# Two fixed PSUM tiles for the divided projections, and the recurrence's key columns scaled on VectorE

## The chip, the cores and the metric

The kernel runs on one core of one Trainium2 chip. The core has five engines that run their own instruction streams and meet at semaphores: TensorE (PE in the profile; its weight loads are listed apart as PEld), VectorE (DVE), ScalarE (ACT), GpSimd (POOL) and SyncE (SP), which here issues transfers. The metric is the device time of one execution in microseconds (us), lower is better; the figure compared is the median of several runs.

## The reference

One inference step of a one-layer streaming encoder for 512 prompt frames and 32 frames of a running stream, all in fp32. What matters here is the HGRN2 half of the mixer:

```
proj = x @ w_in                                  # hq, hf, hi, hg: 8 heads of 128 columns each
f = lb + (1 - lb) * sigmoid(hf);  k = 1 - f      # forget gate and key
S_t = diag(f_t) S_{t-1} + k_t outer v_t          # v = hi
o_t = S_t^T q_t                                  # q = hq
o = rms_norm(o) * silu(hg)
...                                              # latent attention, w_out, ConvFFN with w_up, w_gate, w_down
```

## The kernel before, in words

All activations stand with features on the 128 partitions and the T = 544 frames along the free dimension. An fp32 product is made from three reduced-precision passes: a weight is split into a high part `wh` (ACT copy) and a low part `wl` (DVE subtraction), an activation into `aH` and `aL`, and `wh*aH`, `wh*aL`, `wl*aH` are added up in PSUM.

The projections of heads 2 to 7 are **divided**: the two column groups of a call (query and forget gate, or value and gate, 128 columns each), the two halves of the 2048 input features and the two halves of the frames (NI = 272) make a 2x2x2 block product, done with seven products instead of eight. A call of `divided` (L749) runs the products in the order `ORDER` = 11, s1, s2, s4, s3, 12, 22. Each is 8 k-tiles x 3 passes = 24 matmuls of 272 columns, about 3 us of PE. There are 12 calls, c = 4 to 15 (an even c is a head's query and forget gate, the next odd c its value and gate). Products 11, s2, s3, 22 accumulate into `x`, products s1, s4, 12 into `y`, so consecutive products always alternate between the two. Each accumulator's running value is **taken** (`take`, L755) after each product: for 11, s1, s2 and 22 by an ACT copy (L758), for s4, s3 and 12 by a DVE addition (L761). `x` and `y` are the two halves, each in a 2 KB PSUM bank of its own, of one tile [128, 1024] that `main_tile()` gives anew in each call; there are two such buffers, so calls alternate between them.

The order of work on PE, DVE and ACT is written out by hand in this stage (`tc.manual_schedule`, L948); GpSimd's and SyncE's is not. Per product, in program order: ACT makes `wh` of the product after next (`begin`, L716), PE runs k = 0 to 3, then `settle()` issues the take of the *previous* product, then DVE makes `wl` of the product after next (L721) and often a difference of two weight blocks for the one after that (L711), then a **slot** opens for side work, PE runs k = 4 to 7, and a second slot opens. So a call has 14 slots, a head 28.

The side work is the recurrence of the head before. `levels(h)` (nine steps, about every 1.75 slots) does a doubling scan with block widths m = 1, 2, ..., 64: at each level PE multiplies the scaled keys `Kp` with the scaled queries `Qp` into a PSUM tile `s` (L836 to L841), then the upper half blocks of `Qp` are multiplied by the block totals on DVE (L842), the lower half blocks of `Kp` on GpSimd (L844), the totals are multiplied pairwise on DVE (L850), and the masked scores are copied on DVE (L854) or ACT (L852). The next level's matmuls need the new `Qp` and `Kp`. `finish(h)` (11 steps, one per slot) transposes keys and values (L870), builds the states (L880 to L894), multiplies (L902, L904), squares on ACT (L907), sums on DVE (L911, L912), takes a power on GpSimd (L913), scales on DVE (L916), transposes back (L921) and gates (L923, L925). For heads 0 and 1 the projections are ordinary GEMMs and the same `levels` is woven into them (L939, L940), there outside the hand-written order.

Of the kernel before, what the change touches and what calls it, by code (L numbers as in the profile page):

```python
# [15 lines left out]
P = 128  # L16
# [26 lines left out]
NI = T // 2  # L43
# [16 lines left out]
def tile_encoder_step(ctx, tc, xp, xs, w_in, w_in4, w_kr, w_q_b, w_kv_b, w_out, w_up, w_gate, w_down, w_down2,  # L60
# [3 lines left out]
    V, A, G, PE = nc.vector, nc.scalar, nc.gpsimd, nc.tensor  # L64
# [27 lines left out]
    def main_tile():  # L92
        return psm.tile([P, 1024], F32, name="main", tag="main")
# [54 lines left out]
    def pair_half(ps, j):  # L148
        n = H_[j].stop - H_[j].start
        return [ps[:, 512 * t:512 * t + n] for t in range(2)]  # L150
# [213 lines left out]
    with tc.tile_pool(name="mp", bufs=1) as mp, tc.tile_pool(name="psa", bufs=4, space=PSUM) as psa:  # L364
# [67 lines left out]
        c = {}  # L432
# [207 lines left out]
    with tc.tile_pool(name="gp", bufs=1) as gp, tc.tile_pool(name="psg", bufs=1, space=PSUM) as psg:  # L640
# [83 lines left out]
        def operand(name, k):  # L724
            if name in sums:
                return part(name, k, 0), part(name, k, 1)
            kg, j = {"11": (k, 0), "s3": (k, 1), "12": (HK + k, 0), "22": (HK + k, 1)}[name]
            return aH[kg][:, H_[j]], aL[kg][:, H_[j]]
# [4 lines left out]
        def begin(n):  # L733
            if n < len(products):
                ws_of[n] = products[n][0].high(products[n][1])

        def complete(n):

            if n < len(products):
                ws_of[n] = products[n][0].low(ws_of[n])  # L740
                if n + 1 < len(products):
                    products[n + 1][0].form(products[n + 1][1])

        def settle():
            now, later[:] = later[:], []
            for f in now:
                f()

        def divided(c, a, b, after):  # L749

            ps = main_tile()
            x, y = ps[:, :NI], ps[:, 512:512 + NI]
            t0, t1 = H_

            def take(name, out):  # L755
                kept = {"11": a[:, t0], "s1": b[:, t1], "s2": b[:, t0], "22": a[:, t1]}.get(name)
                if kept is not None:
                    A.activation(kept, out, AF.Copy)  # L758
                else:
                    z = {"s4": b[:, t0], "s3": b[:, t1], "12": a[:, t0]}[name]  # L760
                    V.tensor_tensor(out=z, in0=z, in1=out, op=ALU.add)  # L761
                    if name != "12":
                        after(z)

            for i, name in enumerate(ORDER):
                n = 7 * (c - N_PLAIN) + i
                begin(n + 2)
                wh, wl = ws_of.pop(n)
                out = x if name in ("11", "s2", "s3", "22") else y
                for k in range(HK):  # L770
                    oh, ol = operand(name, k)
                    for q, (ww, aa) in enumerate(((wh, oh), (wh, ol), (wl, oh))):
                        PE.matmul(out, ww[:, k * P:(k + 1) * P], aa, start=name in ("11", "s1", "12") and k == 0 and q == 0,  # L773
                                  stop=k == HK - 1 and q == 2, skip_group_check=True)
                    if k == 3:
                        settle()
                        complete(n + 2)
                        yield
                later.append(lambda name=name, out=out: take(name, out))
                yield  # L780
# [4 lines left out]
        def divided_qf(h):  # L785
            q, f = hq[h], hf[h] = proj_tile(), proj_tile()

            def forget(z):
                A.activation(z, z, AF.Sigmoid)
                A.activation(z, z, AF.Identity, bias=lb[:, h:h + 1], scale=oml[:, h:h + 1])  # L790
            yield from divided(2 * h, q, f, forget)

        def divided_ig(h):
            i, g = hi[h], hgate[h] = proj_tile(), proj_tile()

            def gate(z):
                e = gp.tile([P, 2, NI], F32, name="sg", tag="sg")[:, 0]
                A.activation(e, z, AF.Sigmoid)
                later.append(lambda: V.tensor_tensor(out=z, in0=z, in1=e, op=ALU.mult))
            yield from divided(2 * h + 1, i, g, gate)  # L800

        def sw_tile():
            return psg.tile([P, 1024], F32, name="sw", tag="sw")

        def s1_tile():
            return psg.tile([P, 512], F32, name="s1", tag="s1", bufs=2)

        def levels(h):
            q, f = hq[h], hf[h]
            at = attnT[h % 2]  # L810
            s0 = gp.tile([P, P], F32, name="s0", tag="s0", bufs=2)
            dma(s0, st_d[h])
            Kp = gp.tile([P, T], F32, name="Kp", tag="Kp", bufs=2)
            Qp = gp.tile([P, T], F32, name="Qp", tag="Qp", bufs=2)
            V.tensor_scalar(out=Kp, in0=f, scalar1=-1.0, scalar2=1.0, op0=ALU.mult, op1=ALU.add)
            V.tensor_tensor(out=Qp, in0=q, in1=f, op=ALU.mult)
            yield
            dps = sw_tile()
            for j, (a, b) in enumerate(TOK):
                t0 = a if j < 4 else TP  # L820
                PE.matmul(dps[:, t0:b], Kp[:, a:b], q[:, t0:b], start=True, stop=True)
            V.copy_predicated(out=at, mask=hm[:, :T], data=dps[:, :T])
            tot = f
            tots = None
            for li, m in enumerate(LEVELS):
                n = T if m <= 16 else TP
                nb = n // (2 * m)
                Qv = Qp[:, :n].rearrange("p (b w m) -> p b w m", w=2, m=m)
                Kv = Kp[:, :n].rearrange("p (b w m) -> p b w m", w=2, m=m)
                Av = at[:, :n].rearrange("p (b w m) -> p b w m", w=2, m=m)  # L830
                Tv = tot[:, :n // m].rearrange("p (b w) -> p b w", w=2)
                ps = s1_tile()
                bt = 64 // m
                for j, (a, b) in enumerate(TOK[:5 if m <= 16 else 4]):
                    if m == 64:
                        PE.matmul(ps[:64, j * 64:(j + 1) * 64], Kp[:, a:a + 64], Qp[:, a + 64:b], start=True, stop=True)  # L836
                    elif j < 4:
                        PE.matmul(ps[:, j * 64:(j + 1) * 64], Kp[:, a:b], Qv[:, j * bt:(j + 1) * bt, 1, :],  # L838
                                  start=True, stop=True)
                    else:  # L840
                        PE.matmul(ps[:, 256:272], Kp[:, a:b], Qv[:, 4 * bt:nb, 1, :], start=True, stop=True)  # L841
                V.tensor_tensor(out=Qv[:, :, 1, :], in0=Qv[:, :, 1, :], in1=Tv[:, :, 0:1].to_broadcast([P, nb, m]),  # L842
                                op=ALU.mult)
                G.tensor_tensor(out=Kv[:, :, 0, :], in0=Kv[:, :, 0, :], in1=Tv[:, :, 1:2].to_broadcast([P, nb, m]),  # L844
                                op=ALU.mult)
                if m == 16 or m == 64:
                    nt = gp.tile([P, 32], F32, name="totk", tag=f"tot{m}", bufs=2)
                else:
                    nt = gp.tile([P, 272], F32, name="tot", tag="tot", bufs=2)
                V.tensor_tensor(out=nt[:, :nb], in0=Tv[:, :, 0], in1=Tv[:, :, 1], op=ALU.mult)  # L850
                if m == 64:
                    A.activation(Av[:64, :, 1, :], ps[:64, :256].rearrange("p (b m) -> p b m", m=m), AF.Copy)  # L852
                else:
                    V.copy_predicated(out=Av[:, :, 1, :],  # L854
                                      mask=hm[:, T + 272 * li:T + 272 * li + n // 2].rearrange("p (b m) -> p b m", m=m),
                                      data=ps[:, :n // 2].rearrange("p (b m) -> p b m", m=m))
                if m == 16:
                    tots = nt
                tot = nt
                yield  # L860
            rec[h] = Kp, Qp, tot, tots, at, s0
# [82 lines left out]
        for n in range(2):  # L944
            begin(n)
            complete(n)
        last_finish = finish(HEADS - 1)
        with tc.manual_schedule(engines=MANUAL):  # L948

# [50 lines left out]
    def acc_tile():  # L1000
        seq[0] += 1
        if seq[0] % 2:
            return main_tile()
        return psA.tile([P, 1024], F32, name="acc", tag="acc")
# [349 lines left out]
    for g in (5, 6, 7):  # L1354
# [3 lines left out]
        if g < 7:  # L1358
            ps = pair_half(acc_tile(), 0)
# [218 lines left out]
    with tc.manual_schedule():  # L1578
# [26 lines left out]
        ps = pair_half(acc_tile(), 0)  # L1605
# [81 lines left out]
        for p in range(2, BP):  # L1687
            x = Pair(p)
# [553 lines left out]
```

## Time and profile before

| | |
|---|---|
| median of 3 runs | 2451.21 us (2450.78 to 2453.78) |
| profiled execution, its own time | 2452.24 us |
| its span, first to last instruction | 2450.5 us |
| PE busy | 2354.3 us (96% of the span) |
| DVE busy | 1812.1 us (74%) |
| ACT busy | 1045.2 us (43%) |
| POOL busy | 191.5 us (8%) |
| mean granted TensorE clock | 0.991 |

The own time has 1.7 us that lie outside the span; the profiled execution is 1.0 us above the median. Busy time is the union of an engine's instruction rows; PE rows overlap, because matmuls are pipelined. The divided stage, which the change is about, lies between 380.7 and 775.7 us of the span.

### The profile page before, as it was taken

The numbers are of one execution on the slowest core, as the hardware profiler recorded it, in microseconds if no ns is written. First come the engines' busy times: TensorE is split into PE (matmuls) and PEld (weight loads), VectorE is DVE, ScalarE is ACT, GpSimd is POOL, SyncE is SP. The second block draws the span as 40 slices with busy tenths as digits, with TensorE's granted clock in tenths as the row PEclk, the third lists the DMA queues.
The fourth block names the chain that finished last, engine by engine and source line by source line (L and its number), as shares of the span: only waits on it lengthen the run. The fifth ranks groups of instructions, "written<-read, shape, count | busy, mean of one in ns | idle before, by whom it ended". The sixth has DMA issues, their size and how long they took to land.

```text
span 2450.5 us, 44455 instructions
## 1 busy us (share of the span) xinstructions
PE 2354.3 (96%) x18462; PEld 2317.5 (95%) x18462; DVE 1812.1 (74%) x2447; ACT 1045.2 (43%) x1615; POOL 191.5 (8%) x219
## 2 busy tenths in 40 slices
PE   6999999888899999989999999999999999999997
PEld 6999999888888999989999999999999999999996
DVE  7445577666667546799888888888777888888566
ACT  4244433333334224656555555555444433333234
POOL 4010020111111020000000000000000100000023
PEclk9999999999999999999999999999999999999998
DMA  7232163222224433644535253534333874633322
GB/s 231 91 97 65 62 200 95 70 77 69 73 76 145 170 101 124 204 135 161 174 119 184 102 191 112 177 127 164 117 117 118 313 300 170 224 133 94 115 70 74
DMA packets 131914, 333.21 MB, mean 136 GB/s; under 512 B 11904, under 2 KB 64896, under 8 KB 127104
## 3 DMA queue, kind: packets, MB, share of 16 engines
q1 hardware_dynamic: 122448, 286.91, 35.6%
q0 software_dynamic: 5040, 39.00, 4.0%
q10 hardware_dynamic: 4224, 4.46, 0.5%
q8 instruction: 145, 2.38, 0.4%
q14 instruction: 57, 0.47, 0.1%
HBM read 272.78 MB, written 56.15 MB: 134 GB/s over the span
## 4 chain that ended last, share of the span: by engine, by line
PE 75%; DVE 6%; ACT 2%; issue 2%; POOL 0%; DMA 0%; ACTq 0%; SPq 0%; DVEq 0%
PE main L1217 20%; PE acc L1217 16%; PE main L773 9%; PE main L1245 8%; PE main L118 7%; PE acc L1245 6%; PE acc L118 5%; PE s L838 1%; DVE wl L1169 1%; ACT hproj L758 1%; ACT wh L716 0%; DVE wl L721 0%; DVE hproj L761 0%; ACT zb L1337 0%; PE sw L902 0%
## 5 line engine op out<-in xcount | busy, mean ns | idle before, releaser
L1168 ACT ACTIVATE wh<-raw 128x1024 fp32r<-128x1024 f32 x340 | 359.9, 1059 | 415.0 <-DVE raw L1161 134.4
L1169 DVE TENSOR_TENSOR wl<-raw,wh 128x1024 fp32r<-128x1024 f32 x340 | 415.8, 1223 | 133.9 <-ACT wh L1168 133.0
L1217 PE MATMUL main<-op,wh 128*128 128x272 f32 x1408 | 265.7, 288 | 0.0
L1217 PE MATMUL acc<-ops,wh 128*128 128x272 f32 x1344 | 255.7, 289 | 4.3 <-DVE ops L1298 4.3
L1217 PE MATMUL main<-ops,wh 128*128 128x272 f32 x1344 | 254.2, 287 | 0.0
L1217 PEld LDWEIGHTS main<-op,wh 128*128 128x128 f32 x1408 | 221.0, 188 | 0.0
L1217 PEld LDWEIGHTS acc<-ops,wh 128*128 128x128 f32 x1344 | 212.1, 189 | 4.6 <-DVE ops L1298 4.6
L1217 PEld LDWEIGHTS main<-ops,wh 128*128 128x128 f32 x1344 | 211.0, 188 | 0.0
L1217 PE MATMUL main<-op,wl 128*128 128x272 f32 x704 | 203.1, 288 | 0.9 <-DVE wl L1169 0.9
L1217 PE MATMUL acc<-ops,wl 128*128 128x272 f32 x672 | 194.3, 289 | 0.0
L1217 PE MATMUL main<-ops,wl 128*128 128x272 f32 x672 | 193.8, 288 | 0.2 <-DVE wl L1169 0.2
L118 PE MATMUL main<-aL,wh 128*128 128x272 f32 (+2 forms) x768 | 180.1, 292 | 4.6 <-POOL aL L269 4.6
L118 PE MATMUL main<-aH,wh 128*128 128x272 f32 (+2 forms) x768 | 183.4, 296 | 1.1 <-ACT x L267 0.7
L118 PE MATMUL main<-aH,wl 128*128 128x272 f32 (+2 forms) x768 | 178.9, 291 | 0.0
L107 DVE TENSOR_TENSOR wl<-raw,wh 128x1024 fp32r<-128x1024 f32 (+2 forms) x80 | 89.9, 1127 | 102.9 <-ACT wh L106 97.9
L1217 PE MATMUL acc<-op,wh 128*128 128x272 f32 x832 | 159.8, 290 | 1.6 <-DVE eg L1441 1.6
L1168 ACT ACTIVATE wh<-rawl 128x1024 fp32r<-128x1024 f32 x93 | 98.5, 1060 | 105.8 <-DVE rawl L1161 42.1
L1161 DVE TENSOR_TENSOR raw<-raw,raw 128x1024 f32<-128x1024 f32 x114 | 139.2, 1221 | 1.8 <-DMA raw<-in_w_up 0.2
L773 PE MATMUL main<-aH,wh 128*128 128x272 f32 x384 | 118.2, 308 | 22.6 <-DVE hproj L761 22.6
L1169 DVE TENSOR_TENSOR wl<-rawl,wh 128x1024 fp32r<-128x1024 f32 x93 | 113.8, 1223 | 32.7 <-ACT wh L1168 32.4
L106 ACT ACTIVATE wh<-raw 128x1024 fp32r<-128x1024 f32 (+2 forms) x80 | 75.5, 949 | 140.2 <-PE acc L118 65.6
L118 PEld LDWEIGHTS main<-aL,wh 128*128 128x128 f32 x768 | 129.6, 191 | 5.8 <-POOL aL L269 5.7
(421 smaller groups left out, 6162.0 us busy)
## 6 DMA issues: line engine op xcount, KB each, us to landing
raw<-in_w_in SPq DMA_DIRECT2D x76, 512.0 KB, 3.6
raw<-in_w_up SPq DMA_DIRECT2D x72, 512.0 KB, 4.6
raw<-in_w_gate SPq DMA_DIRECT2D x72, 512.0 KB, 4.0
raw<-in_w_down SPq DMA_DIRECT2D x71, 512.0 KB, 4.1
raw<-in_w_out SPq DMA_DIRECT2D x40, 512.0 KB, 3.5
opd<-ohl SPq DMA_DIRECT2D x16, 1088.0 KB, 5.5
ops<-opd POOLq DMA_DIRECT2D x16, 1088.0 KB, 9.7
opd<-ohl SPq DMA_DIRECT2D x16, 816.0 KB, 6.4
```

The lines of the kernel that those rows point to most:

```text
L106: A.activation(dst(hv), src(rv), AF.Copy)
L107: V.tensor_tensor(out=dst(lv), in0=src(rv), in1=dst(hv).bitcast(F32), op=ALU.subtract)
L118: PE.matmul(ps, ww[:, wcols[0]:wcols[1]], aa[:, hs[j]], start=first and i == 0, stop=last and i == 2, skip_group_check=True)
L758: A.activation(kept, out, AF.Copy)
L773: PE.matmul(out, ww[:, k * P:(k + 1) * P], aa, start=name in ("11", "s1", "12") and k == 0 and q == 0, stop=k == HK - 1 and q == 2, skip_g ...
L838: PE.matmul(ps[:, j * 64:(j + 1) * 64], Kp[:, a:b], Qv[:, j * bt:(j + 1) * bt, 1, :], start=True, stop=True)
L1161: V.tensor_tensor(out=out, in0=a, in1=b, op=ALU.subtract)
L1168: A.activation(wh, src, AF.Copy)
L1169: V.tensor_tensor(out=wl, in0=src, in1=wh.bitcast(F32), op=ALU.subtract)
L1217: PE.matmul(ps, ww[:, k * P:(k + 1) * P], aa, start=self.first and k == 0 and i == 0, stop=k == n - 1 and i == 2, skip_group_check=True)
L1245: PE.matmul(banks[:, 512 * u:512 * u + NI], ww[:, (u * n + k) * P:(u * n + k + 1) * P], aa, start=self.first and k == 0 and i == 0, stop=k ...
```

## The change

```diff
         def divided(c, a, b, after):
-            ps = main_tile()
-            x, y = ps[:, :NI], ps[:, 512:512 + NI]
+            x, y = (banks[(c + i) % 2][:, :NI] for i in range(2))
             t0, t1 = H_
...
                 V.tensor_tensor(out=Qv[:, :, 1, :], in0=Qv[:, :, 1, :], in1=Tv[:, :, 0:1].to_broadcast([P, nb, m]),
                                 op=ALU.mult)
-                G.tensor_tensor(out=Kv[:, :, 0, :], in0=Kv[:, :, 0, :], in1=Tv[:, :, 1:2].to_broadcast([P, nb, m]),
+                V.tensor_tensor(out=Kv[:, :, 0, :], in0=Kv[:, :, 0, :], in1=Tv[:, :, 1:2].to_broadcast([P, nb, m]),
                                 op=ALU.mult)
...
         for n in range(2):
             begin(n)
             complete(n)
+        banks = [main_tile() for i in range(2)]
         last_finish = finish(HEADS - 1)
```

Two things change. First, the accumulators of all 12 calls are the first halves of two tiles that are allocated once, ahead of the stage. `x` of call c is in tile c mod 2 and `y` in the other, so `x` and `y` of one call stand in different tiles, and the bank that holds `y` in one call holds `x` in the next; products alternate between the two banks across the calls too. Second, the multiplication of `Kp` at each level (L844) is a DVE instruction, between the multiplication of `Qp` (L842) and that of the totals (L850); `Kv[:, :, 0, :]` are the lower half blocks of `Kp`. Nothing else moves: the number of matmuls, the transfers and the order of the other instructions in the hand-written stage stay.

## Prediction

> **What bounds the kernel now.** First the page, for the bounding engine, then the stage of the change by windows, then its waits, last single rows in order of time.
>
> ```profile
> PE 2354.3 (96%) x18462; PEld 2317.5 (95%) x18462; DVE 1812.1 (74%) x2447; ACT 1045.2 (43%) x1615; POOL 191.5 (8%) x219
> 380.70:775.70 395.00, 353.03 (x2748) 338.55 (x2746) 271.60 (x388) 143.14 (x214) 53.10 (x49) 0.99 0.27 84
> PE main L773 <- DVE hproj L761: 22.6, 23, 2.5
> PE main L773 <- ACT hproj L758: 17.9, 31, 1.0
> ```
>
> PE is busy 96% of the span, so time comes only from PE's idle stretches or from a shorter stream. In the divided stage (second line: length, then PE, PEld, DVE, ACT, POOL busy, clock) PE idles 42.0 of 395 us, and the two waits, in microseconds, count and longest, make 40.5 of that: 54 times PE's next product matmul waits for a take. Which take, the rows tell:
>
> ```profile
> 480.54 0.41 PE L773 MATMUL main<-s,wh 128*128 128x272 f32 x2
> 480.79 0.29 PE L773 MATMUL main<-s,wl 128*128 128x272 f32 x1
> 481.11 0.40 ACT L758 ACTIVATE hproj<-main 128x272 f32<-128x272 f32 x1 [2.15 <-PE main L773]
> 481.56 0.52 PE L773 MATMUL main<-s,wh 128*128 128x272 f32 x2 [0.49 <-ACT hproj L758]
> 481.92 0.29 PE L773 MATMUL main<-s,wl 128*128 128x272 f32 x1
> 477.52 0.29 PE L773 MATMUL main<-aH,wh 128*128 128x272 f32 x1
> 477.64 0.37 ACT L758 ACTIVATE hproj<-main 128x272 f32<-128x272 f32 x1
> 477.65 0.29 PE L773 MATMUL main<-aL,wh 128*128 128x272 f32 x1
> ```
>
> The first five rows are the middle of product s1: PE has run k = 0 to 3 into `y`, ACT takes product 11 out of `x`. Two banks, no shared data, yet ACT starts only when PE's last matmul into `y` ends, having idled 2.15 us while 11 lay ready, and PE goes on only when ACT is done. The last three rows are the natural experiment: the take of 22 falls into the next call, whose 11 goes to the *other tile*, and PE does not pause. So the waits hang on the tile, not on the bank or the value.
>
> **The change part by part.** *Two tiles.* Neighbouring products then always stand in different tiles, as 22 and the next 11 do now, so the mid-product stop has nothing left to wait for. What one costs: 480.79 to 481.92 is 1.13 us for three matmuls that take 0.375 undisturbed (480.54 to 480.79 is two in 0.25, so 0.125 each). That is 0.755, 0.27 more than the 0.49 listed as idle, as the pipeline drains and refills. For 54 stops: 40.5 + 54 x 0.27 = 55.1 us.
>
> What is late next is the DVE chain that made the longest stops; they come once per head, five times:
>
> ```profile
> 474.24 0.40 PE L773 MATMUL main<-aH,wh 128*128 128x272 f32 x1 [2.50 <-DVE hproj L761]
> ...
> 740.44 0.40 PE L773 MATMUL main<-aH,wh 128*128 128x272 f32 x1 [2.51 <-DVE hproj L761]
> 466.45 0.71 ACT L907 ACTIVATE sqg<-sw 128x640 f32<-128x640 f32 x1 [2.76 <-PE sw L904]
> 467.06 1.05 ACT L716 ACTIVATE wh<-raw 128x1024 fp32r<-128x1024 f32 x1
> 468.32 1.22 DVE L721 TENSOR_TENSOR wl<-raw,wh 128x1024 fp32r<-128x1024 f32 x1
> 473.01 0.82 DVE L916 TENSOR_TENSOR sqg<-sw,r 128x640 f32<-128x640 f32 x1 [1.28 <-POOL r L913]
> 475.35 1.23 DVE L711 TENSOR_TENSOR raw<-raw 128x1024 f32<-128x1024 f32 x1
> 475.85 0.71 PE L921 MATMUL sw<-ident,sqg 128*128 128x128 f32 x5
> 476.31 0.37 PE L773 MATMUL main<-aH,wh 128*128 128x272 f32 x1
> 476.67 1.06 ACT L716 ACTIVATE wh<-raw 128x1024 fp32r<-128x1024 f32 x1 [4.78 <-DVE raw L711]
> 477.76 2.45 DVE L721 TENSOR_TENSOR wl<-raw,wh 128x1024 fp32r<-128x1024 f32 x2 [0.26 <-ACT wh L716]
> 481.27 0.43 DVE L815 TENSOR_SCALAR Kp<-hproj 128x544 f32<-128x544 f32 x1
> ```
>
> I set both chains at 466.2, where PE begins product 12, and run them on without the stops. DVE's weight subtraction cannot start before the ACT copy ends at 468.1, so the chain to L916 moves only 0.2 earlier and ends near 473.6. PE needs four half products of 12 x 0.125 = 1.5 us and is through 22 at 472.3; its transposes L921 read what L916 writes: a stop of 1.35. They take about 0.46 (475.85 to 476.31), so 11 runs from 474.1 to 477.15. Now s1 wants the bank that 22 filled, a wait the old alternation of tiles did not have. The take of 22 stands on ACT behind L716, which waits for L711: all 0.2 earlier than now, so done at 477.85, a stop of about 0.75. Product s1 ends at 480.9; the recurrence's first matmuls need `Kp` from L815, now at 481.1 to 481.5: 0.6 more. Put back: 2.7 per head, 13.5 for five.
>
> *`Kp` on DVE.* Rows of the divided stage, by shape (busy, mean ns of one, idle before):
>
> ```profile
> L844 POOL TENSOR_TENSOR Kp<-Kp,tot 128x272 f32<-128x272 f32 (+1 forms) x30 | 31.8, 1060 | 90.0 <-PE s L841 75.9 <-PE s L836 14.1
> L842 DVE TENSOR_TENSOR Qp<-Qp,hproj 128x272 f32<-128x272 f32 x6 | 2.7, 443 | 2.0 <-PE s L841 2.0
> L850 DVE TENSOR_TENSOR tot<-hproj 128x272 f32<-128x272 f32 x6 | 6.8, 1132 | 0.0
> L850 DVE TENSOR_TENSOR tot<-tot 128x136 f32<-128x136 f32 x6 | 4.7, 786 | 0.0
> L850 DVE TENSOR_TENSOR tot<-tot 128x68 f32<-128x68 f32 x6 | 3.9, 648 | 0.0
> L850 DVE TENSOR_TENSOR tot<-tot 128x34 f32<-128x34 f32 x6 | 4.0, 669 | 0.0
> L850 DVE TENSOR_TENSOR totk<-tot 128x17 f32<-128x17 f32 x6 | 1.0, 168 | 0.0
> 500.32 0.44 DVE L842 TENSOR_TENSOR Qp<-Qp,tot 128x272 f32<-128x272 f32 x1 [1.74 <-PE s L841]
> 500.68 0.67 DVE L850 TENSOR_TENSOR tot<-tot 128x34 f32<-128x34 f32 x1
> 505.06 0.43 DVE L842 TENSOR_TENSOR Qp<-Qp,tot 128x272 f32<-128x272 f32 x1
> 505.85 1.00 PE L838 MATMUL s<-Qp,Kp 128*128 128x64 f32 x8
> ```
>
> Seven levels of six heads add 42 DVE instructions like L842, each 0.36 from its start to the next one's (500.32 to 500.68) to 0.44 long: 15.1 to 18.5 us. Against that L850, which runs beside L844 now, loses its stretch: the 272-wide one takes 1132 ns where L842 of that width takes 443, so 4.1 us come back; the three narrower ones must lie between 443 and the 168 of width 17, which gives (786 + 648 + 669 - 3 x 443) x 6 = 4.6 to 9.6 us. Net on DVE +1 to +10 us, spread over 395 - 272 = 123 us of DVE idle: cover enough on average. The Trainium skill, SBUF (SBUF: two separate sides), states that a DVE instruction with two SBUF inputs and a GpSimd one that reads SBUF exclude each other for the whole instruction; this trace agrees as far as the 1132 against 443 ns go.
>
> On the path, `Kp` must be ready for the next level's matmuls. GpSimd needs 1.06 us per scaling; DVE has `Kp` 0.36 + 0.44 after its own start, so it is sooner where DVE is free. Where it is late it is tight: the `Qp` row at 505.06 ends 0.36 ahead of the matmuls at 505.85, and `Kp` behind it would just arrive. There the shorter L850 and no L844 beside L711 bring DVE forward too, so I take 0.3 us per head, 1.5 in all; the ends are 0 and 0.36 at each of 6 x 6 hand-overs, 13 us. The 14 instructions of heads 0 and 1 lie ahead of the stage, outside these rows; by their 0.3 us each way I set them at nothing, with ends of -2 and +2.
>
> *The clock.* Windows of two successive heads and around one stop (clock is the third number from the end):
>
> ```profile
> 448.51:514.25 65.74, 58.02 (x455) 55.60 (x455) 44.77 (x64) 22.39 (x33) 8.80 (x8) 1.00 0.24 72
> 514.25:581.58 67.33, 59.61 (x455) 57.19 (x455) 44.63 (x64) 22.39 (x33) 8.81 (x8) 0.97 0.23 70
> 538.00:541.60 3.60, 1.61 (x12) 1.61 (x13) 2.80 (x4) 0.00 (x0) 0.73 (x1) 1.00 0.00 0
> 541.60:545.00 3.40, 3.40 (x18) 3.40 (x17) 2.81 (x5) 2.29 (x3) 0.00 (x0) 0.50 0.09 34
> 674.70:678.10 3.40, 3.40 (x17) 3.40 (x16) 2.79 (x5) 2.29 (x3) 0.00 (x0) 0.50 0.07 28
> ```
>
> Same work, 1.6 us apart: after two of the five long stops (PE busy 1.61 of 3.60) the clock is at 0.50 for 3.4 us. With stops of 1.35 instead of 2.5 I expect neither: 3.2 us; the ends are 0 and 3.2. The Trainium skill, TensorE: Matmul & The Clock Gate (What's actually happening), says the gate halves the clock after an idle window of about 3.4 us, in windows that run free of the program. By full idleness alone no stop here would have tripped it; the half-idle 3.60 us at 538.00 did, so the trace is stricter than that sentence. By it the two dips do not hang on these stops and would stay, which gives 2411 in place of 2408.
>
> **The sum.** 55.1 - 13.5 - 1.5 + 3.2 = 43.3 us off the profiled execution's own 2452.2 gives 2408.9; the median shown is 1.0 below that execution, so 2408.
>
> **The rivals.** *Full release*: the chain behind L916 keeps up because ACT and DVE are no longer held for PE. For it: DVE idles 123 us. Against: that chain is already packed. 2451.2 - 55.1 - 3.2 = 2393, with one of the three stops left about 2397. *`Kp` late*: DVE's order puts `Kp` behind takes and weight subtractions that GpSimd never waited for, and each hand-over costs its 0.36 (13 us), with the dips kept (3.2): 2408 + 11.5 + 3.2 = 2423. For it: the row at 505.06. The Trainium skill, TensorE: Matmul & The Clock Gate (Architectural detail), calls DVE's queue strictly first in, first out; the trace's rows are in program order too, so that lateness cannot be overtaken. *Nothing changes*: the waits are not the tile's. Against it stand the unpaused takes of 22; 2451. *Slower*: PE ahead of DVE turns each hand-over into a stop. With 43.3 us to lose over 36 hand-overs it decides from 1.2 us each; at one L721 plus `Kp`, 1.22 + 0.36 = 1.58, it is 57 us and 2465. Against: of PE's 42.0 idle us now, 40.5 are the takes, so no hand-over stops PE for more than a trace of that time.
>
> **How the numbers follow.** Forecast (2400 to 2416) 0.55; full release (below 2400) 0.13; late `Kp` (2416 to 2432) 0.24; nothing 0.04; slower 0.04. A measurement here tells from no change about 0.2%, 5 us: faster 0.93, same 0.04, slower 0.03 (a little of the last case falls short of 5 us). The range 2396 to 2428 leaves out some 0.17.
>
> **What the changed profile would show.** Takes beside running matmuls within a call, and the two waits of L773 from 54 times to some ten, mostly ACT L758 at about 0.75; L921 waiting for L916 about 1.3 us per head, five times; no L844 on POOL; L850 of width 272 at 0.43; no half clock near the heads' ends. Wrong would be: the 0.49 us stops still there (the tile is not the cause), L838 waiting for `Kp` L844 in most levels (late `Kp`), or wl or wh named ahead of L773 (the weights' chain becomes the bound).

## The result, and the profile after

The changed kernel takes 2406.84 us (median of 4 runs, 2405.20 to 2408.31) against 2450.99 us for the kernel before on the same occasion: a ratio of 0.982, 95% interval 0.9803 to 0.9837. The forecast was 2408, with a range of 2396 to 2428. Three single runs in the experiments, of 4365, 5664 and 7582 us, are left out of the medians given below.

Line numbers in `divided` and behind it are one lower now, so the products are L772, the takes L757 and L760, the scaling of the keys L843, the transposes back L920. First the page, then windows (heads 0 and 1, the divided stage, the stretch behind it; the last three columns are PE clock, DMA share and GB/s), then who PE waited for in the divided stage (total us, times, longest).

```profile
span 2405.8 us, 44402 instructions
PE 2341.0 (97%) x18462; PEld 2315.4 (96%) x18462; DVE 1805.3 (75%) x2503; ACT 1044.4 (43%) x1615; POOL 131.6 (5%) x163
```

```profile
309.80:377.50 67.70, 67.27 (x557) 66.20 (x555) 54.89 (x137) 22.89 (x47) 1.29 (x1) 1.00 0.57 181
377.50:725.60 348.10, 336.10 (x2733) 331.48 (x2732) 263.06 (x428) 141.32 (x212) 6.99 (x6) 1.00 0.30 95
725.60:760.40 34.80, 31.24 (x239) 30.57 (x237) 21.26 (x34) 10.56 (x16) 1.17 (x1) 0.95 0.51 173
```

```profile
PE sw L920 <- DVE sqg L915: 6.7, 5, 1.3
PE sw L820 <- DVE Kp L814: 2.5, 5, 0.5
PE main L772 <- ACT hproj L757: 2.0, 5, 0.4
```

The same three stages of the kernel before, which the prediction showed only in part:

```profile
311.10:380.90 69.80, 67.63 (x553) 66.05 (x551) 56.55 (x125) 23.97 (x48) 15.44 (x15) 1.00 0.57 178
380.90:774.90 394.00, 352.40 (x2743) 338.18 (x2743) 270.80 (x387) 142.34 (x212) 52.90 (x49) 0.99 0.27 84
774.90:806.80 31.90, 28.95 (x231) 28.03 (x229) 18.53 (x30) 9.30 (x13) 1.17 (x1) 1.00 0.57 190
```

The span is 44.7 us shorter. The divided stage gives 394.0 - 348.1 = 45.9 of it, heads 0 and 1 ahead of it 2.1, the start of the kernel 1.3; the 32 us behind the stage lose 2.9 and the rest of the kernel 1.7. The 54 stops for takes became five of 0.4 us, and two waits come once per head, five times each: the transposes' wait for the scaled tile, which the kernel before had once (1.1 us, at the start of the stage), and the wait of the levels' first matmuls, which it had nowhere. A take within a call now looks as the take of 22 did before (this is product 11 taken during s1; the weight loads are left out of the timeline):

```profile
465.53 0.41 PE L772 MATMUL main<-s,wh 128*128 128x272 f32 x2
...
465.77 0.29 PE L772 MATMUL main<-s,wl 128*128 128x272 f32 x1
...
465.84 0.39 ACT L757 ACTIVATE hproj<-main 128x272 f32<-128x272 f32 x1
465.90 0.41 PE L772 MATMUL main<-s,wh 128*128 128x272 f32 x2
```

PE goes on in steps of 0.125 us through the ACT copy. And this is the chain that is late, at the same place as in the prediction:

```profile
459.99 0.82 DVE L915 TENSOR_TENSOR sqg<-sw,r 128x640 f32<-128x640 f32 x1 [1.34 <-POOL r L912]
460.73 0.43 DVE L760 TENSOR_TENSOR hproj<-hproj,main 128x272 f32<-128x272 f32 x1
460.87 0.77 PE L920 MATMUL sw<-ident,sqg 128*128 128x128 f32 x5 [1.34 <-DVE sqg L915]
463.65 1.06 ACT L716 ACTIVATE wh<-raw 128x1024 fp32r<-128x1024 f32 x1 [4.84 <-DVE raw L711]
464.61 0.38 ACT L757 ACTIVATE hproj<-main 128x272 f32<-128x272 f32 x1
465.05 0.52 PE L772 MATMUL main<-s,wh 128*128 128x272 f32 x2 [0.39 <-ACT hproj L757]
468.25 0.44 DVE L814 TENSOR_SCALAR Kp<-hproj 128x544 f32<-128x544 f32 x1
468.84 1.27 PE L820 MATMUL sw<-hproj,Kp 128*128 128x128 f32 x10 [0.51 <-DVE Kp L814]
```

The last group shows the keys on DVE, by shape (busy, mean ns):

```profile
L843 DVE TENSOR_TENSOR Kp<-Kp,tot 128x272 f32<-128x272 f32 x24 | 10.5, 436 | 0.0
L849 DVE TENSOR_TENSOR tot<-hproj 128x272 f32<-128x272 f32 x6 | 2.6, 435 | 0.0
L849 DVE TENSOR_TENSOR tot<-tot 128x34 f32<-128x34 f32 x6 | 1.1, 190 | 0.0
```

The product of totals of width 272 went from 1132 to 435 ns, that of width 34 from 669 to 190.

### The profile page after: what moved, and what is told of

The parts are those of the page before. It is cut to its first block, busy times and chain, and to the rows that moved or that the text cites. A ratio compares the mean times of both kernels' runs of the same rounds, so it can differ in the third digit from the quotient of the medians.

```text
span 2405.8 us, 44402 instructions
## 1 busy us (share of the span) xinstructions
PE 2341.0 (97%) x18462; PEld 2315.4 (96%) x18462; DVE 1805.3 (75%) x2503; ACT 1044.4 (43%) x1615; POOL 131.6 (5%) x163
## 4 chain that ended last, share of the span: by engine, by line
PE 88%; DVE 6%; ACT 2%; issue 1%; DMA 1%; POOL 0%; ACTq 0%; DVEq 0%; POOLq 0%; SPq 0%
PE main L1217 20%; PE acc L1217 16%; PE main L118 16%; PE main L772 8%; PE main L1245 8%; PE acc L1245 6%; PE acc L118 5%; PE s L837 2%; DVE wl L721 1%; DVE raw L711 1%; PE at L600 1%; PE main L540 1%; PE at L570 1%; PE at L571 1%; DVE wl L1169 1%
## 5 line engine op out<-in xcount | busy, mean ns | idle before, releaser
L1168 ACT ACTIVATE wh<-raw 128x1024 fp32r<-128x1024 f32 x340 | 359.9, 1060 | 415.2 <-DVE raw L1161 134.3
L1169 DVE TENSOR_TENSOR wl<-raw,wh 128x1024 fp32r<-128x1024 f32 x340 | 415.8, 1223 | 134.5 <-ACT wh L1168 133.6
L721 DVE TENSOR_TENSOR wl<-raw,wh 128x1024 fp32r<-128x1024 f32 x84 | 103.1, 1228 | 49.6 <-ACT wh L716 49.1
L716 ACT ACTIVATE wh<-raw 128x1024 fp32r<-128x1024 f32 x84 | 88.7, 1056 | 114.8 <-DVE raw L711 109.9
L1169 DVE TENSOR_TENSOR wl<-rawl,wh 128x1024 fp32r<-128x1024 f32 x93 | 113.7, 1223 | 32.7 <-ACT wh L1168 32.6
```

What stands on the lines that cost most here:

```text
L716: A.activation(wh, self.src, AF.Copy)
L721: V.tensor_tensor(out=wl, in0=self.src, in1=wh.bitcast(F32), op=ALU.subtract)
L1168: A.activation(wh, src, AF.Copy)
L1169: V.tensor_tensor(out=wl, in0=src, in1=wh.bitcast(F32), op=ALU.subtract)
```

## The experiments

All times are medians; the kernel before ran beside each group at 2451.8, 2452.5 and 2452.0 us. The changed kernel ran only on the occasion above, beside 2451.0, so a difference from its 2406.84 us can carry the 1.5 us or so by which those four differ. Diffs are against the changed kernel; lines are cut short at "...".

**The two tiles alone.** The change without its second part:

```diff
-                V.tensor_tensor(out=Kv[:, :, 0, :], ...
+                G.tensor_tensor(out=Kv[:, :, 0, :], ...
```

> The two fixed tiles alone; the key columns are scaled on GpSimd as before. Theory (the gain is the mid-product stops, and those hang on x and y sharing a tile): nearly the whole gain is here, 2407 to 2412 us; what is missing are the 2.0 us that heads 0 and 1 became shorter and at most some 3 us of DVE instructions stretched beside GpSimd. The takes of a call overlap with running product matmuls, and PE waits for a take about five times, not 54. Rival (the gain comes from DVE being freed of GpSimd's instructions): 2425 to 2440, with PE waiting for DVE in the levels.

Measured 2407.03 us, ratio 0.9815 (0.9802 to 0.9828): all of the gain. The three waits of the changed kernel are there with nearly the same lengths (the sixth at L920 is the one of 1.1 us that the kernel before has too), and no wait for GpSimd:

```profile
381.10:730.00 348.90, 336.90 (x2736) 332.05 (x2735) 267.02 (x384) 139.40 (x210) 52.71 (x49) 1.00 0.30 94
```

```profile
PE sw L920 <- DVE sqg L915: 7.5, 6, 1.3
PE sw L820 <- DVE Kp L814: 2.5, 5, 0.5
PE main L772 <- ACT hproj L757: 2.0, 5, 0.4
```

The divided stage is 348.9 us long against 348.1. DVE is busy 267.0 us with the keys on GpSimd and 263.1 with them on DVE: 42 instructions more, yet 4 us less, because the others run unstretched. That the total is no higher than the changed kernel's, though the keys' move is worth about 3 us (last experiment but one), goes with the clock. This profile lacks the two half-clock windows that the changed kernel has behind the stage (paragraph on the clock below), though it has one of its own in heads 0 and 1 (323.4 to 326.8, at 0.51). At the same mean clock, 0.993, the changed kernel's one such run took 2405.20 us and three of this kernel took 2406.62 to 2407.84.

**The keys alone.** The kernel before with the keys on DVE:

> The key columns on DVE alone; x and y are halves of one tile per call as before. Theory: PE keeps its 54 stops for takes (about 40 us idle in the divided stage), and only heads 0 and 1 get about 2 us shorter: 2446 to 2451 us. Rival (DVE freed of GpSimd's instructions is the gain): 2420 to 2435.

Measured 2448.76 us, ratio 0.9986 (0.9978 to 0.9995), about 3 us. Heads 0 and 1 take 67.7 us (before 69.8), the divided stage 393.7 (before 394.0), with 53 of its 54 stops:

```profile
377.50:771.20 393.70, 352.65 (x2742) 339.08 (x2740) 266.19 (x430) 144.08 (x214) 7.00 (x6) 0.99 0.26 84
```

```profile
PE main L773 <- DVE hproj L761: 22.6, 22, 2.6
PE main L773 <- ACT hproj L758: 17.7, 31, 1.0
```

**Two banks of one tile.** The changed kernel, its two banks from one tile:

```diff
-        banks = [main_tile() for i in range(2)]
+        one = main_tile()
+        banks = [one[:, 512 * i:512 * i + 512] for i in range(2)]
```

> As the changed kernel, with the same alternation of two banks over all calls, but the two banks are the halves of one tile. Theory (the stop hangs on the shared tile): all 84 takes stop PE or hide behind side work, the takes of product 22 too, which did not stop it in the kernel before: the 55 us come back and up to 11 stops of 0.75 us with them, 2452 to 2462 us. Rival (different banks are enough; what helped was that the banks alternate over the calls): 2405 to 2409, as the changed kernel.

Measured 2454.34 us, ratio 1.0009 (1.0 to 1.0018), and the stops are back, now 59 of them:

```profile
PE main L772 <- DVE hproj L760: 22.5, 22, 2.6
PE main L772 <- ACT hproj L757: 20.7, 37, 1.0
```

Six more for ACT are the takes of 22, which now share the running product's tile too. The stage is 401.3 us long, 7.3 more than in the kernel before: besides the stops it has five half-clock windows where that one has two. Two banks alternate as in the changed kernel, and the gain is gone: the wait hangs on the tile. This is the experiment that decides. What no run separates is a tile from the place of its banks: the halves of one tile are next to each other, and the accumulators of the changed kernel, first halves of two tiles, are not. Against the place as the cause stands that the profile infers these waits from semaphore events, ACT released by PE's last matmul and PE by ACT; a run with neighbouring banks in two tiles is missing.

**The keys written twice.** One more DVE instruction per level:

```diff
                 V.tensor_tensor(out=Kv[:, :, 0, :], in0=Kv[:, :, 0, :], in1=Tv...
+                V.tensor_tensor(out=Kv[:, :, 0, :], in0=Kv[:, :, 0, :], in1=Kv[:, :, 0, :], op=ALU.max)
```

> As the changed kernel, with one more DVE instruction per level, behind the scaling of the key columns: their maximum with themselves, in place, which leaves the values as they are. DVE gets 42 x 0.36 to 0.44 = 15 to 18 us more in the divided stage, and every level has its keys 0.36 to 0.44 us later. Theory (DVE has cover there): 2407 to 2412. Rival (the hand-over of the keys is at its edge, the prediction's case of late keys): 36 hand-overs x 0.36 = 13 us or more, 2420 to 2428.

Measured 2413.94 us, 7.1 more than the changed kernel: between the two ranges, so both missed. DVE is busy 281.7 us in the stage, 18.6 more, and the stage is 357.0 us long, 8.9 more. Waits that the changed kernel does not have appear between levels, 4.7 us in these two rows:

```profile
378.00:735.00 357.00, 338.54 (x2732) 332.08 (x2731) 281.70 (x471) 142.48 (x213) 7.00 (x6) 1.00 0.30 93
```

```profile
PE s L835 <- DVE tot L850: 2.9, 6, 0.5
PE s L837 <- DVE Kp L845: 1.8, 5, 0.4
```

So DVE's 85 us of idle time in the stage hide only half of this addition, which stands between the new keys and the matmuls that want them. That the change itself shows no such wait fits its adding nothing to DVE on balance, and is no sign of deep cover. This run both loads DVE and delays the keys, and which of the two PE paid for is not shown.

**The transposes back one slot later.** One more `yield` ahead of L919, and 12 steps for `finish` instead of 11:

> As the changed kernel, with the transposes back at the end of finish (which wait 1.34 us per head for the scaled tile) one slot later, in the middle of the next call's product 11. Theory (one DVE chain sets the pace there: power on GpSimd, scaling L915, take of 12, two weight instructions, weight copy, two more, first keys; the transposes' wait is only where it shows first): nothing is gained, 2405 to 2409 us; PE waits about as long for the take of 12 instead. Rival (the transposes' own order is the fault): 5 x 1.34 = 7 us faster, about 2400.

Measured 2414.61 us, 7.8 more than the changed kernel; both expectations missed. Nothing was gained, as the theory said, and the wait changed its name as it said, but it got longer:

```profile
PE main L772 <- DVE hproj L760: 8.9, 5, 1.8
PE main L1027 <- DVE n_e L1038: 5.0, 1, 5.0
PE sw L820 <- DVE Kp L814: 3.7, 3, 1.2
```

The divided stage became 4.3 us longer, 352.4 against 348.1, and it has two half-clock windows, which the changed kernel's stage has not:

```profile
521.50:524.90 3.40, 3.40 (x18) 3.40 (x17) 2.18 (x3) 1.88 (x3) 0.00 (x0) 0.50 0.00 0
699.00:702.40 3.40, 3.40 (x18) 3.40 (x17) 2.21 (x2) 2.23 (x3) 0.00 (x0) 0.50 0.00 0
```

At 1.7 us each, an estimate (half of 3.4 us), they are 3.4 of the 4.3, so the waits themselves cost only about 0.9 us more than those they replace. Behind the stage the second row of the waits is the main part: the last head's `finish` has a step more as well, and the norm behind the output projection waits 5.0 us where it waited 1.2.

**The levels one slot later.**

```diff
-                beside_from(s0, levels(h), 9, ...
+                beside_from(s0 + (h < HEADS - 1), levels(h), 9, ...
```

> As the changed kernel, with the levels of heads 2 to 6 one slot later. Theory (the first keys are the end of the same DVE chain and only 0.5 us late): the wait of the levels' first matmuls goes, 0.5 us per head, and the waits for the scaled tile and for the take of 22 stay: 2403 to 2407 us, unless the later slots bring new waits between levels. Rival (the levels' place is the cause of the waits before it too): 2395 to 2400.

Measured 2401.40 us, 5.4 less than the changed kernel and between the two ranges. The levels' wait fell from 2.5 to 0.5 us, the other two stayed at 6.8 and 2.0, and the stage is 345.3 us, 2.8 less; that is the size of the theory's wait, 5 x 0.5 us. Of the rest a part is the clock: this kernel's profile has neither of the changed kernel's two half-clock windows behind the stage (below), and at the same mean clock, 0.993 and 0.992, its runs are 3.8 and 4.0 us below the changed kernel's. The remaining 1 us or so is not explained.

**Finish one slot earlier.**

```diff
-                    beside_from(s0 + 15, finish(h), 11, 1)
+                    beside_from(s0 + 14, finish(h), 11, 1)
```

> As the changed kernel, with finish of heads 2 to 6 one slot earlier, so that its sum, power and scaling stand on DVE ahead of the weight instructions they stand behind now, and the take of 12 is no longer behind the scaling. Theory (that DVE chain is what is late): all three waits of a head go (1.34 + 0.39 + 0.50 idle, 11 us with five heads): 2394 to 2398 us. Rival (DVE is at its limit there whatever the order): the wait moves to another instruction, 2403 to 2409.

Measured 2389.10 us, ratio 0.9744 (0.9729 to 0.9759), and once more in another group 2389.24, 0.9746 (0.9733 to 0.976): 17.7 and 17.6 us below the changed kernel, more than either expectation.

```profile
377.10:710.60 333.50, 332.67 (x2734) 331.18 (x2733) 263.31 (x428) 143.05 (x212) 7.00 (x6) 1.00 0.31 99
```

```profile
PE sw L869 <- DVE og L924: 0.8, 1, 0.8
PE sw L920 <- DVE sqg L915: 0.2, 1, 0.2
```

```profile
456.15 0.82 DVE L915 TENSOR_TENSOR sqg<-sw,r 128x640 f32<-128x640 f32 x1
457.55 0.71 PE L920 MATMUL sw<-ident,sqg 128*128 128x128 f32 x5
```

All three waits are gone; PE is busy 332.7 of 333.5 us, and the transposes start 0.6 us after the scaling has ended. The stage itself is 333.3 us long (the window above is 0.2 us wider), 14.8 shorter than in the changed kernel. Of these, 11.2 are listed as idle there; the other 3.6 over 15 stops are 0.24 a stop, near the 0.27 that the prediction read as lost beside a listed row. Beyond that its first profile lacks the changed kernel's two half-clock windows behind the stage. DVE was late by order, not by load: its busy time is the same 263.

**Finish earlier, the transposes not.** Finish one slot earlier with the additional step:

> As the kernel with finish one slot earlier, and the transposes back left where they stand in the changed kernel (one slot more between scaling and transposes). Theory: there is no wait left for this to remove, so the same as that kernel, 2394 to 2398 us. Rival (the scaling is still late for the earlier transposes): 3 to 6 us faster than that kernel.

Measured 2396.18 us: inside the theory's range, but 7.1 above the kernel that it was to equal, so neither expectation holds. In the stage there was indeed nothing left to remove (334.0 us against 333.3). The loss is behind it, where the additional step again delays the last head: the norm waits 3.6 us instead of 1.2, and its profile has half clock for 10.2 us in two places right behind the stage. How the 7.1 us divide between these is not settled.

**Finish earlier, the keys on GpSimd.** What the second part of the change is worth when PE has no other wait:

> The two fixed tiles and finish one slot earlier, with the key columns scaled on GpSimd as in the kernel before; against the kernel with finish earlier and keys on DVE (2389.1 us) it tells what the keys' move is worth once no other wait is left in the stage. Theory (the move is neutral in the divided stage, since what DVE gains in instructions it loses in stretched ones, and is worth 2 us in heads 0 and 1): 2389 to 2393 us, no wait for GpSimd above 2 us in the stage. Rival (with the slack gone, DVE instructions stretched beside GpSimd bring waits back): 2396 to 2405.

Measured 2391.97 us (2391.89 to 2394.99), as the theory said, against 2389.24 for its twin with the keys on DVE in the same group.

```profile
309.60:379.40 69.80, 67.59 (x553) 66.00 (x551) 56.57 (x125) 23.98 (x48) 15.43 (x15) 1.00 0.56 179
379.40:713.80 334.40, 333.27 (x2737) 331.55 (x2736) 267.19 (x384) 141.13 (x210) 52.73 (x49) 1.00 0.31 99
```

```profile
PE sw L920 <- DVE sqg L915: 1.1, 1, 1.1
```

Heads 0 and 1 take 69.8 instead of 67.5 us, the stage 334.4 instead of 333.3. So the keys' move is worth about 3 us: 2.7 by the medians, 3.4 by these two lengths, most of it outside the stage that the rest of the change is about. Within the stage one wait of 1.1 us is left at its start, which is 0.2 with the keys on DVE.

> The kernel with finish one slot earlier once more, as the measure for the one above on the same chip: 2387 to 2391 us; if the gain over the changed kernel hangs on where half-clock windows fall, its profile shows other windows after the stage and the time moves by 1.7 us for each.

The twin's stage is again 333.3 us; its profiled span is 3.2 us longer than the first one's, which the last section explains.

## Why the prediction was right

**The cause.** The wait of a take on the running product's tile was read from two groups of rows, a take within a call and one across calls. Two banks of one tile bring it all back, two tiles take it all away.

**The size.** Taking away all stops and both half-clock windows was put at 55.1 + 3.2 = 58.3 us. The kernel with finish one slot earlier, which has hardly a wait left, shows it: 394.0 - 333.3 = 60.7, its keys on DVE included. Counting the 0.27 us a stop beside the listed idle time mattered; the listed idle time alone would have said 40.5.

**What is late next.** Three stops per head were worked out from the rows; measured are 1.34 at the transposes (forecast 1.35), 0.39 at the bank that 22 filled (0.75) and 0.50 at the first keys (0.6). Put back were 13.5 + 1.5 us; measured 348.1 - 333.3 = 14.8. That these agree so closely is luck: the 14.8 belong to the three stops, put at 13.5, and the 1.5 for the hand-overs to nothing. That one chain makes all three, and that it is an order and not a load, the kernel with finish one slot earlier shows.

**The keys.** The hand-overs were given 1.5 us; the changed kernel has no wait there. The net on DVE was put between +1 and +10 us and is -4 between the two kernels with two tiles: instructions other than L850 that run beside GpSimd's had been stretched too, which the sum had left out (the weight differences L711 had a mean of 1317 ns and have 1223; the 256-wide multiplications of `Qp` by `tot` had 768 and have 420). *Late keys* was the right thing to fear, as the doubled instruction shows, at two thirds of the 13 us that the prediction put on it: 8.9 us in the stage. Heads 0 and 1 were set at nothing with ends of -2 and +2; they gained 2.1.

**The clock.** Both half-clock windows of the stage are gone, as forecast, but the changed kernel has two behind it that the kernel before has not:

```profile
730.80:734.20 3.40, 3.40 (x18) 3.40 (x18) 3.40 (x5) 0.00 (x0) 0.00 (x0) 0.50 0.08 7
761.60:765.00 3.40, 3.40 (x17) 3.40 (x16) 0.15 (x1) 0.40 (x1) 0.00 (x0) 0.51 1.06 399
```

The kernel before had one at 807.8 in their place. So of the 3.2 us expected one window's 1.7 came back, and that is the larger part of the 2.9 us lost behind the stage; the rest of it is not traced. That the forecast came within 1.2 us is in part luck: the stage gave 2.6 us more than the 43.3 of the sum, and of what the sum left at nothing, heads 0 and 1 and the start gave 3.4 while the stretches behind the stage took 4.6.

**The chances.** The 0.93 for faster is 0.01 more than its three cases add up to (0.55 + 0.13 + 0.24).

## What to carry to other kernels

Where an accumulator is read while the next one is filled, look whether the reader starts only when the writer pauses: if two banks of one tile do that, give each bank a tile of its own. After removing a regular stop, run the rows of the next slowest engine forward by hand to find where it is late, and first try to move its work one slot ahead before taking work off it: here that took 14.8 us off the stage for one number, and taking instructions off GpSimd brought about 3. Idle time of an engine over a stage is no cover for work added at a fixed place in it; half of what was added showed.

## What the runs showed of the hardware that had not been expected

A stop's price is not its idle row: 0.49 us listed cost 0.755 from matmul to matmul. The prediction had counted that from one stop; the same reading of the rows at all 54 stops gives 0.27 us more than listed on average.

Windows of 3.4 us at half clock need no fully idle stretch: in the kernel before, PE was busy 2.17 of the 3.40 us ahead of the one at 807.8. Within one execution their starts lie on one grid: 541.6, 674.7 and 807.8 are 133.1 us apart, 39 times 3.413 (a window's length in the traces), and the five in the kernel with two banks of one tile are 68.3 apart, 20 times 3.413. That bears on why only two of the five long stops in the kernel before were followed by a dip: each of the five lies across a boundary of the grid, and the 3.4 us that hold the larger part of it have 1.61 and 1.58 us of PE work ahead of the two dips, 1.84, 1.83 and 1.83 in the other three cases (from 469.9, 603.0 and 736.1). PE's busy time alone does not decide, as the 2.17 shows, and no run moves a stop along the grid, so this reading is not proved.

Where the windows fall changes from execution to execution. The same kernel, finish one slot earlier, over the same times in its two profiles, the second run first:

```profile
715.90:719.30 3.40, 3.34 (x16) 3.04 (x16) 3.40 (x5) 0.00 (x0) 0.00 (x0) 0.50 0.07 10
746.60:750.00 3.40, 3.40 (x18) 3.40 (x17) 0.22 (x1) 0.40 (x1) 0.00 (x0) 0.50 1.06 392
```

```profile
715.90:719.30 3.40, 2.31 (x20) 2.12 (x19) 3.40 (x6) 0.00 (x0) 0.00 (x0) 1.00 0.23 19
746.60:750.00 3.40, 3.40 (x30) 3.40 (x29) 2.07 (x5) 1.18 (x3) 0.86 (x1) 1.00 1.06 400
```

In one they run at 0.50, in the other at full clock, and the spans are 2389.0 and 2385.8 us with a stage of 333.3 us in both. Differences of 2 or 3 us between kernels that differ in one stage are therefore read from the stage's length, with the half-clock windows in it counted, not from the total.

The Trainium skill, TensorE: Matmul & The Clock Gate (What's actually happening), names an idle window of about 3.4 us, free of the program's start. That the windows fall differently in two executions agrees with the second half; the first half does not cover this kernel, where 1.61 us of work in 3.60, and 2.17 in 3.40, did not keep the clock up.
